# Seven 1 MB weight buffers instead of four in the expert stage of a two-block kernel

## The chip, the cores and the metric

The kernel runs on one core of one Trainium2 chip. The metric is the device time of one launch in microseconds (us), lower is better. Three runs of the kernel before gave 2560.94, 2565.24 and 2565.53 us, median 2565.24 us.

## The reference, cut to what matters

Two blocks follow each other on 256 tokens of width 1024, everything in float32. The first block has two attentions, a cross attention and, at its end, a mixture of experts: 32 experts in 4 groups, 2 experts per token.

```
x = x + cross_attention(...)
hm = rms_norm(x, g_ffn)                      # 256 x 1024
group, two experts of it per token, weights  # the routing
y[e] = (silu(xb @ w_gate[e]) * (xb @ w_up[e])) @ w_down[e]   # 1024 -> 512 -> 1024, 32 experts
x = x + sum over the two experts of weight * y
```

The second block works on two sequences of 256 rows, the tokens (the first block's result) and a context, which does not depend on the first block at all. Per layer of two: a gated feed-forward (1024 to 2816 to 1024), a mixer (layer 0: recurrent mLSTM plus spatial gating; layer 1: window attention, whose keys and values come partly from the context), and a second feed-forward. The context stops after its keys and values of layer 1. Scales and shifts of each step come from a modulation, `silu(c) @ ada_w`.

## The kernel before, in words

Two instruction streams are recorded and then woven into one order per engine by a scheduler at compile time. `fore` is first block, routing, experts, and then the second block's token rows. `back` is the modulation weights and the context rows. Names of tiles begin with f or b after their stream. The scheduler simulates the program with its own timing and takes, among what it thinks is ready, the instruction with the lowest priority number; a stream's number is a start plus a slope times the matmul work done so far (`SEG`, line 1832). The resulting order is fixed: each engine runs its row in that order and waits on semaphores. The queue that issues all weight loads is SP's, and it too is strictly in order: a load that waits for its buffer holds up every load behind it, of either stream.

A `fore` load is 128 x 2048 floats, 1 MB, into one of the `raw` buffers (`FORE`, raw=4). A `back` load is 128 x 1024 floats, 0.5 MB, into one of five. Dense layers take float32 apart: ScalarE copies 512 columns of the raw buffer into a rounded part (tag `sph`), VectorE (for `fore`) or GpSimd (for `back`) subtracts to get the rest (tag `spl`), and TensorE does three fp32r matmuls per 128 x 128 block. A raw buffer is free again when the subtraction has read it. A 0.5 MB load of `back` feeds 24 matmuls of 256 columns.

The experts do without that: their weights go from the raw buffer straight into float32 matmuls, so an expert buffer is free when TensorE has read it (lines 1190 to 1219). Four experts of a group are done together, 32 token slots each, in 8 groups. A group is 16 loads of gate and up weights, a gate function, four transposes, 8 loads of down weights, and a combine that adds the result to `xres`. Gathers of the next tokens stand between groups. After group `SPILL` there is one extra expert with 6 loads. That is 198 loads of 1 MB. Behind the experts stands a loop for further extra experts (`tc.For_i`, line 1306), which runs zero times with these inputs; it splits the program, and what the scheduler puts ahead of it stays ahead of it.

The tags `sph`, `spl`, `q1`, `dg`, `ld`, `rope` and `wg` (splits, rotary tables, attention pieces, narrow weights) are used by the first block before the routing and by the token rows behind the loop, not by the experts. Before the change they have memory of their own throughout.

The stages in the profile: first block and routing to about 451 us, experts 451 to 1316, the loop, then on the token rows a feed-forward (full rate from 1383 to 1546), the mixer of layer 0 (to about 1817), two feed-forwards (to 2182), the window attention, and the last feed-forward.

Of the kernel before, what the change touches and what calls it, by code (L numbers as in the profile page):

```python
# [39 lines left out]
class X2:  # L40


    def __init__(self, h, l, both=None):
        self.h, self.l, self.both = h, l, both
# [27 lines left out]
class Stream:  # L72
    def __init__(self, K, es, name, bufs, ps_bufs, unit):
        self.K, self.name, self.bufs = K, name, bufs
        self.pool = es.enter_context(K.tc.tile_pool(name=name, bufs=1))
        self.pp = es.enter_context(K.tc.tile_pool(name=name + "p", bufs=ps_bufs, space=PSUM))
        self.n = self.ada = self.lows = 0
        self.sq = None
        self.pool_low = LOW.get(name)
        self.unit = unit  # L80
        self.chain, self.side = {}, {}
        self.seg(0, 1)

    def seg(self, start, slope):

        self.start, self.slope, self.done = start, slope, 0.0
# [8 lines left out]

    def t(self, tag, shape, dt=F32):
        self.n += 1
        return self.pool.tile(shape, dt, tag=tag, bufs=self.bufs[tag], name=f"{self.name}{tag}{self.n}")

    def parts(self, n=T):  # L100

# [56 lines left out]
class Kern:  # L158
    def __init__(self, tc, I, dbg=None):
        self.tc, self.real, self.I, self.dbg = tc, tc.nc, I, dbg  # L160
        self.nc = Engines(self, tc.nc)
        self.cur = self.stream = None
        self.p0 = tc.cur_priority
        self.after = {}

    def link(self, key, r):
        if self.cur is None:
            return
        for prev in (self.cur.get(key), self.after.pop(key, None)):
            if prev is None:  # L170
                continue
            self.tc.add_manual_dep(
                r.ins, prev, mybir.DependencyInfo(mybir.DependencyClass.NoSync, mybir.DependencyReason.DATA),
                reason="stream order")
        self.cur[key] = r.ins.name
# [20 lines left out]
    def pair(self, S, src):  # L196

        if S.unit == 2048:
            raw = self.load(S, src)
            return raw[:, :1024], raw[:, 1024:]  # L200
        return [self.load(S, src[:, i * 1024:(i + 1) * 1024]) for i in range(2)]

    def misc(self, S, tag, shape, src, dt=F32):
        t = S.t(tag, shape, dt)
        self.real.gpsimd.dma_start(t, src)
        return t
# [824 lines left out]
    def moe(self, S):  # L1031
# [7 lines left out]
        xx = S.t("xx", [128, 2, 2, 1024], F32R)  # L1039
# [12 lines left out]
        def ct(n):  # L1052
            used[0] += n
            return scratch[:, used[0] - n:used[0]]
# [23 lines left out]
        dg = ct(8).rearrange("p (b n) -> p b n", b=2)  # L1078
# [58 lines left out]
        def onehot(base, n, b, shift=None):  # L1137
            d = S.t("c", [128, 2])
            if shift is None:
                ts(d, dest[:, :, b], -float(base), None, op0=OP.add)  # L1140
            else:
                tt(d, dest[:, :, b], shift.to_broadcast([128, 2]), op=OP.subtract)
            o, f = S.t("k1", [128, n], F32R), S.t("k1", [128, n])
            ts(f, iota[:, :n], d[:, 0:1], None, op0=OP.is_equal)
            stt(o, iota[:, :n], d[:, 1:2], f, op0=OP.is_equal, op1=OP.add)
            return o
# [13 lines left out]
        def combine(py, s):  # L1160

            o, ws = s
            Yh, Yl = S.t("k4", [128, 1024], F32R), S.t("k4", [128, 1024], F32R)
            for i in range(2):
                q = slice(i * 512, (i + 1) * 512)
                self.split_to(Yh[:, q], Yl[:, q], py[i], ws)
            for d in range(0, KC, 2):
                p = S.ps([128, 2, T])
                for i in range(2):
                    q = slice((d + i) * 128, (d + i + 1) * 128)  # L1170
                    self.mm(p[:, i], Yh[:, q], o, True, False)
                    self.mm(p[:, i], Yl[:, q], o, False, True)
                nc.vector.tensor_tensor(xres[:, d:d + 2], xres[:, d:d + 2], p, op=OP.add)

        wg, wu, wd = I["w_eg"], I["w_eu"], I["w_ed"]

        def gather(pair):
            P = [onehot(256 * pair, 256, b) for b in range(2)]
            xg = [S.t("k4", [128, 4, T]) for _ in range(2)]
            for k in range(0, KC, 2):  # L1180
                p = S.ps([128, 2, T])
                for i in range(2):
                    q = slice((k + i) * 128, (k + i + 1) * 128)
                    for b in range(2):
                        self.mm(p[:, i], hm[b][0][:, q], P[b], b == 0, False)
                        self.mm(p[:, i], hm[b][1][:, q], P[b], False, b == 1)
                nc.scalar.activation(xg[k // 4][:, k % 4:k % 4 + 2], p, AF.Copy)
            return xg

        def experts_in(grp, xg):  # L1190
            g = grp % 2
            pg = [S.ps([128, 512]) for _ in range(2)]
            for k in range(KC):
                raws = [self.load(S, wt[grp, k]) for wt in (wg, wu)]
                for s in (1, 0):
                    for j in range(4):
                        self.mm(pg[s][32 * j:32 * j + 32],
                                xg[k // 4][:, k % 4, g * 128 + 32 * j:g * 128 + 32 * j + 32],
                                raws[s][:, j * 512:(j + 1) * 512], k == 0, k == KC - 1)
            a = self.gated(S, pg[0], 512)  # L1200
            stt(a, a, 0.5, pg[1], op0=OP.mult, op1=OP.mult)
            return a

        def experts_out(grp, a):
            pt = S.ps([128, 512])
            for c in range(4):
                nc.tensor.transpose(pt[:, c * 128:(c + 1) * 128], a[:, c * 128:(c + 1) * 128], self.ident)
            hT = S.t("k2", [128, 4, 128])
            nc.scalar.activation(hT.rearrange("p a b -> p (a b)"), pt, AF.Copy)
            py = [S.ps([128, 512]) for _ in range(2)]  # L1210
            for c in range(4):
                raws = [self.load(S, wd[grp, 2 * c + i]) for i in range(2)]
                for i in (1, 0):
                    for j in range(4):
                        self.mm(py[i][32 * j:32 * j + 32], hT[:, c, 32 * j:32 * j + 32],
                                raws[i][:, j * 512:(j + 1) * 512], c == 0, c == 3)
            slot = S.t("c", [128, 1])
            ts(slot, self.cst[:, C_PCOL:C_PCOL + 1], 128.0 * grp, None, op0=OP.add)
            combine(py, scatter(slot))

        xg = gather(0)

        ta, tb = S.t("k2", [128, 16, 32]), S.t("k2", [128, 16, 32])
# [69 lines left out]
        for grp in range(8):  # L1293
            a = experts_in(grp, xg)
            if grp % 2 == 1 and grp < 7:
                xg = gather(grp // 2 + 1)
            experts_out(grp, a)
            if grp == SPILL:
                spill(sync.value_load(ti[0:1, 0:1], min_val=0, max_val=7),
                      sync.value_load(ti[0:1, 16:17], min_val=0, max_val=3))  # L1300

        self.moe_load = S.chain["sync"]

        n_more = self.real.values_load(ti[0:1, 32:33], min_val=0, max_val=15)
        keep_chain, self.cur = self.cur, None
        with tc.For_i(0, n_more) as it:
# [516 lines left out]


SPILL = 4
DEFER = 0
PLAN = {-1: 'rrr', 0: 'r', 6: 'r', 8: 'raak'}
PLAN_N = 32
CUT = ((0, 9, 9, 9, 9), (0, 3, 3, 3, 3))
FORE = dict(raw=4, sph=3, spl=3, xx=1, k1=6, k2=4, k4=6, c=16, q1=4, dg=2, ld=1, dst=6, wg=2, gc=5, c72=1, rope=1)  # L1830
BACK = dict(raw=5, sph=3, spl=3, xh=1, xl=1, k1=4, k2=4, k4=3, c=16, q1=2, wg=1, gc=4, c72=1)
SEG = dict(c1b=(1150, 2), first=(-5000, 1), ada=(0, 0), c0a=(300, 1.25), c0b=(530, 1.3), c0c=(680, 1.3), ada1=(950, 3), c1a=(1050, 4.8),
           route=(-5000, 1), moe=(365, 2.6), tok=(1050, 1.38))
# [3 lines left out]
def kernel(ctx: ExitStack, tc: tile.TileContext, I, out, dbg=None, stop=None):  # L1837
    K = Kern(tc, I, dbg)
    nc = K.nc
    fore = Stream(K, ctx, "f", FORE, 5, 2048)  # L1840
    back = Stream(K, ctx, "b", BACK, 3, 1024)
    K.dram = ctx.enter_context(tc.tile_pool(name="dram", bufs=1, space=bass.MemoryType.DRAM))
    K.setup(fore, ctx)

    def context():
# [113 lines left out]
    for c in range(KC):  # L1959
        nc.vector.scalar_tensor_tensor(x[:, c], x[:, c], K.gains[:, 5, c:c + 1], bc, op0=OP.mult, op1=OP.mult)  # L1960
        nc.sync.dma_start(out[:, c], x[:, c])


def _units(w):
# [145 lines left out]
```

## Time and profile before

| | |
|---|---|
| median of three runs | 2565.24 us (2560.94 to 2565.53) |
| the profiled execution | 2558.79 us, its span 2557.0 us |
| TensorE busy / mean granted clock | 93% / 0.964 |
| VectorE, ScalarE, GpSimd busy | 60%, 48%, 29% |
| moved by DMA | 617.23 MB, mean 241 GB/s |

The span is what lies between the first and the last instruction. A busy TensorE is not a TensorE at its peak, since the ends of pipelined matmuls are modelled; the number of matmuls in a stretch (the x in a row) tells more. A DMA share near 1.0 means that the 16 DMA engines have no idle time left.

### The profile page before, as it was taken

What the parts mean: (1) busy time and instruction counts of PE and PEld (TensorE: products, weight loads), DVE (VectorE), ACT (ScalarE), POOL (GpSimd) and SP (SyncE); (2) the same over time, 40 slices, a digit from 0 to 9 for tenths busy, and PEclk for the clock granted to TensorE, in tenths of its full rate; (3) what the DMA queues carried; (4) which work ended last, traced back from release to release, by engine and by line L of the source; (5) the groups of instructions that cost most, each with busy time, mean ns of one, the idle gap of its engine ahead of it and who ended that gap; (6) DMA issues with size and microseconds to landing.
All of it is one profiled execution on the core that took longest, in us unless ns stands there. A gap on an engine that the chain in (4) does not pass through costs nothing. (4 is left out here: it accounts for less than half of the span.)

```text
span 2557.0 us, 46079 instructions
## 1 busy us (share of the span) xinstructions
PE 2373.3 (93%) x17688; PEld 1998.3 (78%) x17688; DVE 1533.7 (60%) x3347; ACT 1228.0 (48%) x2510; POOL 730.0 (29%) x584
## 2 busy tenths in 40 slices
PE   6999998998989999999679999998999899798998
PEld 4767998785666888878348998988899799667897
DVE  6546677235543333352148776767878777677777
ACT  4434554343433433343035555545556555565554
POOL 1000245664524665656141004231000100524000
PEclk9999998999989999999889999999999999899999
DMA  9896543997979898989884554462455355355452
GB/s 373 312 333 255 179 154 132 357 354 293 383 293 364 334 352 306 366 327 343 348 309 168 182 188 142 176 212 103 166 188 191 135 194 182 115 184 197 168 193 102
DMA packets 115231, 617.23 MB, mean 241 GB/s; under 512 B 13232, under 2 KB 14704, under 8 KB 63936
## 3 DMA queue, kind: packets, MB, share of 16 engines
q1 hardware_dynamic: 113616, 610.20, 64.4%
q0 software_dynamic: 1392, 4.06, 0.5%
q8 instruction: 140, 2.29, 0.3%
q14 instruction: 83, 0.68, 0.1%
HBM read 612.11 MB, written 2.10 MB: 240 GB/s over the span
## 5 line engine op out<-in xcount | busy, mean ns | idle before, releaser
L60 POOL TENSOR_TENSOR bspl<-braw,bsph 128x512 fp32r<-128x512 f32 x468 | 608.6, 1309 | 883.3 <-ACT bsph L60 830.4
L60 PE MATMUL fps<-fxx,fsph 128*128 128x512 f32 (+2 forms) x2656 | 734.8, 346 | 19.5 <-DVE fxx L60 10.3
L60 ACT ACTIVATE fsph<-fraw 128x512 fp32r<-128x512 f32 x764 | 479.4, 629 | 483.2 <-PE fps L60 427.9
L60 DVE TENSOR_TENSOR fspl<-fraw,fsph 128x512 fp32r<-128x512 f32 x712 | 498.6, 703 | 234.0 <-ACT fsph L60 216.7
L60 PE MATMUL fps<-fxx,fspl 128*128 128x256 f32 (+1 forms) x2000 | 571.6, 286 | 1.9 <-DVE fspl L60 1.5
L60 PEld LDWEIGHTS fps<-fxx,fsph 128*128 128x128 f32 x2656 | 467.1, 193 | 88.8 <-DVE fxx L60 16.5
L60 ACT ACTIVATE bsph<-braw 128x512 fp32r<-128x512 f32 x468 | 290.9, 629 | 389.9 <-PE bps L60 321.2
L60 PEld LDWEIGHTS fps<-fxx,fspl 128*128 128x128 f32 x2000 | 384.1, 192 | 7.5 <-DVE fspl L60 4.4
L60 PE MATMUL bps<-bxh,bsph 128*128 128x256 f32 x1264 | 363.9, 288 | 5.6 <-ACT bsph L60 3.8
L60 PE MATMUL bps<-bxh,bspl 128*128 128x256 f32 x1264 | 363.7, 288 | 4.2 <-POOL bspl L60 4.0
L60 PE MATMUL bps<-bxl,bsph 128*128 128x256 f32 x1264 | 360.5, 285 | 2.3 <-DVE fk L60 2.2
L60 PE MATMUL fps<-fk,fsph 128*128 128x256 f32 x1632 | 297.8, 284 | 0.0
L60 PEld LDWEIGHTS bps<-bxh,bsph 128*128 128x128 f32 x1264 | 243.5, 193 | 30.6 <-issue 11.9
L60 PEld LDWEIGHTS bps<-bxh,bspl 128*128 128x128 f32 x1264 | 243.1, 192 | 24.6 <-POOL bspl L60 17.3
L60 PEld LDWEIGHTS fps<-fk,fsph 128*128 128x128 f32 x1632 | 254.7, 192 | 3.8 <-issue 0.9
L60 PEld LDWEIGHTS bps<-bxl,bsph 128*128 128x128 f32 x1264 | 243.3, 192 | 10.7 <-issue 8.1
L60 POOL TENSOR_TENSOR fk<-fk,fk 128x512 f32<-128x512 f32 x16 | 21.2, 1323 | 774.2 <-ACT fk L60 769.1
L60 PE MATMUL fps<-fraw,fk 128*32 128x512 f32 (+1 forms) x1600 | 211.2, 642 | 29.9 <-DMA fraw<-in_w_eu_dram 17.9
L60 PE MATMUL fps<-fk,fspl 128*128 128x256 f32 x816 | 230.8, 283 | 0.0
L60 DVE SCALAR_TENSOR_TENSOR bk<-bk,bps 128x256 f32<-128x256 f32 (+1 forms) x148 | 60.3, 411 | 246.9 <-ACT bk L60 244.9
L60 PE MATMUL bps<-bk,bsph 128*128 128x256 f32 x1056 | 198.9, 287 | 3.7 <-DVE bk L60 1.9
L60 PEld LDWEIGHTS bps<-bk,bsph 128*128 128x128 f32 x1056 | 167.6, 194 | 14.0 <-issue 5.9
(351 smaller groups left out, 3203.4 us busy)
## 6 DMA issues: line engine op xcount, KB each, us to landing
fraw<-in_ffn_in_dram SPq DMA_DIRECT2D x88, 1024.0 KB, 4.8
braw<-in_ffn_in_dram SPq DMA_DIRECT2D x132, 512.0 KB, 5.9
fraw<-in_w_eg_dram SPq DMA_DIRECT2D x66, 1024.0 KB, 7.2
fraw<-in_w_eu_dram SPq DMA_DIRECT2D x66, 1024.0 KB, 9.2
fraw<-in_w_ed_dram SPq DMA_DIRECT2D x66, 1024.0 KB, 6.9
fraw<-in_ffn_out_dram SPq DMA_DIRECT2D x44, 1024.0 KB, 4.8
braw<-in_ffn_out_dram SPq DMA_DIRECT2D x66, 512.0 KB, 5.8
braw<-in_ada_w_dram SPq DMA_DIRECT2D x59, 512.0 KB, 7.4
```

Source lines behind the costliest of these rows:

```text
L60: r = f(*args, **kw)
```

## The change

The seven tags move from the stream's pool into a second one that is closed and opened again by phase: "f1" for the first block, "fm" for the experts, "f2" for the token rows. In "fm" the same memory holds three more 1 MB buffers, tag `more`. A new function `expert` replaces `load` in the experts' groups and takes in turn four buffers of `raw` and three of `more`. The extra expert (`spill`) and all else keep `load`. A tile of a later phase waits for the tiles of the earlier one whose memory it takes.

```diff
+    def phase(self, name, tags=()):
+        if self.scope:
+            self.scope.close()
+        self.scope, self.tags = ExitStack(), tags
+        self.extra = self.scope.enter_context(self.K.tc.tile_pool(name=name, bufs=1, side="right", reuse_waits="tile"))
...
+        pool = self.extra if tag in self.tags else self.pool
+        return pool.tile(shape, dt, tag=tag, bufs=self.bufs[tag], name=f"{self.name}{tag}{self.n}")
...
+    def expert(self, S, src):
+        raw = S.t("raw" if self.experts % 7 < 4 else "more", [128, S.unit])
+        self.experts += 1
+        self.nc.sync.dma_start(raw, src)
+        return raw
...
-                raws = [self.load(S, wt[grp, k]) for wt in (wg, wu)]
+                raws = [self.expert(S, wt[grp, k]) for wt in (wg, wu)]
...
-                raws = [self.load(S, wd[grp, 2 * c + i]) for i in range(2)]
+                raws = [self.expert(S, wd[grp, 2 * c + i]) for i in range(2)]
...
+        S.phase("fm", ("more",))
         xg = gather(0)
...
+        S.phase("f2", PHASE)
         n_more = self.real.values_load(ti[0:1, 32:33], min_val=0, max_val=15)
...
+PHASE = ("sph", "spl", "q1", "dg", "ld", "rope", "wg")
```

No arithmetic changes, but the scheduler's simulation comes out otherwise, and with it the order on every engine. Counted in the order of both programs: of `back`'s 0.5 MB loads 300 stand ahead of the loop before and 267 after; of its matmuls 5230 before and 4423 after. `fore` has the same work on both sides of the loop. Behind the loop, `back`'s matmuls up to the first ones of the token mixer are 340 before and 823 after, and within the mixer 585 before and 909 after. From the second token feed-forward on both orders have the same work.

The first place is SP's queue at the first expert loads. Before (braw are loads of the context, fraw those of `fore`; w_eg, w_eu, w_ed are gate, up and down weights of the experts):

```order
L60 DMA fraw_12255<-in_w_eg_dram 128x2048
L60 DMA fraw_12257<-in_w_eu_dram 128x2048
L60 DMA braw_1331<-in_ffn_in_dram 128x1024
L60 DMA fraw_12267<-in_w_eg_dram 128x2048
...
L60 DMA braw_1632<-in_ffn_in_dram 128x1024
L60 DMA fraw_12269<-in_w_eu_dram 128x2048
L60 DMA braw_1634<-in_ffn_in_dram 128x1024
...
L1299 TENSOR_LOAD fdst_12233
```

The same place after:

```order
L60 DMA fraw_12276<-in_w_eu_dram 128x2048
L60 DMA fmore_12286<-in_w_eg_dram 128x2048
L60 DMA fmore_12288<-in_w_eu_dram 128x2048
L60 DMA fmore_12298<-in_w_eg_dram 128x2048
L60 DMA braw_1635<-in_ffn_in_dram 128x1024
...
L1317 TENSOR_LOAD fdst_12240
```

Seven expert loads instead of four stand ahead of the read of the routing result (TENSOR_LOAD), and the three new ones stand ahead of the context's next load.

The second place is SP's queue at the end of the experts. Before:

```order
L60 DMA fraw_14145<-in_w_ed_dram 128x2048
L60 DMA fraw_14147<-in_w_ed_dram 128x2048
L60 DMA braw_14447<-in_ffn_in_dram 128x1024
L60 DMA braw_14449<-in_ffn_in_dram 128x1024
...
L60 DMA braw_14679<-in_ffn_in_dram 128x1024
L1306 COMPARE_AND_BRANCH
```

And after:

```order
L60 DMA fraw_14152<-in_w_ed_dram 128x2048
L60 DMA braw_7716<-in_ffn_in_dram 128x1024
L60 DMA fraw_14154<-in_w_ed_dram 128x2048
L60 DMA braw_7718<-in_ffn_in_dram 128x1024
...
L60 DMA braw_7873<-in_ffn_in_dram 128x1024
L1325 COMPARE_AND_BRANCH
```

Before, the context is through its second feed-forward of layer 0 and has begun with layer 1 (14447 to 14679) when the loop comes; after, it has only begun that second feed-forward of layer 0 (7716 to 7873).

The third place is SP's queue in the first token feed-forward behind the loop. Before:

```order
L60 DMA fraw_15238<-in_ffn_in_dram 128x2048
L60 DMA fraw_15304<-in_ffn_in_dram 128x2048
L60 DMA fraw_15371<-in_ffn_in_dram 128x2048
L60 DMA fraw_15437<-in_ffn_in_dram 128x2048
L60 DMA fraw_15504<-in_ffn_out_dram 128x2048
```

And after:

```order
L60 DMA fraw_15249<-in_ffn_in_dram 128x2048
L60 DMA braw_8339<-in_ffn_out_dram 128x1024
L60 DMA fraw_15315<-in_ffn_in_dram 128x2048
L60 DMA braw_8341<-in_ffn_out_dram 128x1024
L60 DMA fraw_15382<-in_ffn_in_dram 128x2048
```

The rest of the context's feed-forward is now woven into the tokens' one.

## Rows read from the trace of the kernel before

**Rows 1.** The page: TensorE's granted clock and the DMA share, 40 slices, in tenths.

```profile
PEclk9999998999989999999889999999999999899999
DMA  9896543997979898989884554462455355355452
```

**Rows 2.** Busy times by stage (stretch, length, engines' busy time, clock, DMA, GB/s).

```profile
451.00:1316.00 865.00, 796.63 (x6134) 607.40 (x6132) 314.83 (x695) 319.33 (x607) 446.01 (x349) 0.95 0.89 341
1316.00:1357.00 41.00, 33.44 (x247) 31.76 (x248) 34.83 (x71) 22.33 (x44) 29.63 (x22) 0.96 0.61 231
1357.00:1383.00 26.00, 24.43 (x149) 21.13 (x149) 21.53 (x48) 15.57 (x33) 0.94 (x1) 1.00 0.53 183
1383.00:1546.00 163.00, 162.88 (x1082) 149.93 (x1082) 127.60 (x252) 95.89 (x194) 1.49 (x2) 1.00 0.52 183
1546.00:1612.00 66.00, 63.85 (x471) 56.18 (x469) 46.08 (x104) 35.19 (x70) 32.92 (x25) 1.00 0.41 139
1612.00:1735.00 123.00, 118.20 (x951) 107.27 (x952) 83.90 (x197) 66.00 (x129) 31.79 (x29) 0.97 0.55 195
1735.00:1817.00 82.00, 73.23 (x520) 67.37 (x518) 63.08 (x142) 46.11 (x96) 9.23 (x7) 0.94 0.33 116
```

**Rows 3.** The same view, slices of 20 us within the experts.

```profile
600.00:620.00 20.00, 15.97 (x98) 8.33 (x98) 12.61 (x40) 6.36 (x14) 2.28 (x2) 0.83 0.73 286
620.00:640.00 20.00, 18.52 (x119) 13.44 (x117) 15.56 (x33) 9.89 (x19) 8.07 (x7) 0.91 0.60 229
...
700.00:720.00 20.00, 16.13 (x98) 13.59 (x102) 5.23 (x20) 6.49 (x15) 4.24 (x4) 0.74 0.59 234
...
820.00:840.00 20.00, 17.84 (x122) 13.69 (x123) 17.18 (x40) 8.78 (x19) 5.99 (x5) 0.85 0.68 264
...
880.00:900.00 20.00, 20.00 (x168) 16.77 (x164) 6.32 (x11) 8.53 (x16) 14.30 (x12) 1.00 0.97 369
...
980.00:1000.00 20.00, 19.49 (x150) 17.85 (x151) 12.68 (x26) 7.29 (x14) 12.24 (x10) 0.91 0.59 213
...
1100.00:1120.00 20.00, 19.96 (x152) 16.11 (x150) 13.84 (x33) 11.86 (x24) 9.48 (x8) 0.94 0.70 256
...
1220.00:1240.00 20.00, 15.23 (x120) 10.09 (x120) 2.63 (x6) 1.90 (x3) 5.95 (x5) 0.89 0.74 288
...
1260.00:1280.00 20.00, 10.11 (x65) 1.85 (x57) 0.00 (x0) 0.00 (x0) 0.00 (x0) 0.84 1.01 419
1280.00:1300.00 20.00, 12.50 (x64) 2.62 (x68) 3.16 (x10) 1.19 (x2) 0.00 (x0) 0.67 0.93 354
```

**Rows 4.** What SP's queue waited for, 300 to 1320 us (total, times, longest).

```profile
SPq L60 <- POOL bspl L60: 478.0, 159, 11.0
SPq L60 <- PE fps L60: 280.6, 172, 12.6
```

**Rows 5.** The timeline: expert matmuls in the tail (start, length, [idle before <- releaser]).

```profile
1259.29 3.62 PE L60 MATMUL fps<-fraw,fk 128*32 128x512 f32 x16 [3.14 <-DMA fraw<-in_w_eu_dram]
```

**Rows 6.** The timeline: two context matmuls in a full stretch.

```profile
882.02 0.28 PE L60 MATMUL bps<-bxh,bsph 128*128 128x256 f32 x1
882.14 0.28 PE L60 MATMUL bps<-bxl,bsph 128*128 128x256 f32 x1
```

**Rows 7.** The timeline of VectorE: two equal small operations in a row.

```profile
353.90 0.16 DVE L60 SCALAR_TENSOR_TENSOR fc<-fc 128x2 f32<-128x2 f32 x1
354.10 1.25 DVE L60 TENSOR_TENSOR fc<-fc,fc 128x2 f32<-128x2 f32 x1
```

**Rows 8.** GpSimd's subtractions for the context, 1546 to 1750 us (min/median/max ns).

```profile
L60 POOL TENSOR_TENSOR bspl<-braw,bsph x48: 1252/1289/1759, 1548.2 to 1750.0; 128x512 fp32r<-128x512 f32 x48
```

**Rows 9.** The timeline: the first block's last split, and SP's loads beside it.

```profile
382.78 0.33 SPq L60 DMA_DIRECT2D braw<-in_ffn_in_dram  x1
...
383.54 1.35 DVE L60 TENSOR_TENSOR fspl<-fraw,fsph 128x256 fp32r<-128x256 f32 x2
...
384.92 0.33 SPq L60 DMA_DIRECT2D fraw<-in_w_eu_dram  x1
```

More of the change, by code (lines that the diff above doesn't have):

```diff
@@ L77, in __init__ @@
         self.n = self.ada = self.lows = 0
-        self.sq = None
+        self.sq = self.scope = self.extra = None
+        self.tags = ()
         self.pool_low = LOW.get(name)
@@ L97, in t @@
         self.n += 1
-        return self.pool.tile(shape, dt, tag=tag, bufs=self.bufs[tag], name=f"{self.name}{tag}{self.n}")
+        pool = self.extra if tag in self.tags else self.pool
+        return pool.tile(shape, dt, tag=tag, bufs=self.bufs[tag], name=f"{self.name}{tag}{self.n}")
     def parts(self, n=T):
@@ L164, in __init__ @@
         self.after = {}
+        self.experts = 0
     def link(self, key, r):
@@ L1829 @@
 CUT = ((0, 9, 9, 9, 9), (0, 3, 3, 3, 3))
-FORE = dict(raw=4, sph=3, spl=3, xx=1, k1=6, k2=4, k4=6, c=16, q1=4, dg=2, ld=1, dst=6, wg=2, gc=5, c72=1, rope=1)
+FORE = dict(raw=4, sph=3, spl=3, xx=1, k1=6, k2=4, k4=6, c=16, q1=4, dg=2, ld=1, dst=6, wg=2, gc=5, c72=1, rope=1, more=3)
 BACK = dict(raw=5, sph=3, spl=3, xh=1, xl=1, k1=4, k2=4, k4=3, c=16, q1=2, wg=1, gc=4, c72=1)
@@ L1842 @@
     K.dram = ctx.enter_context(tc.tile_pool(name="dram", bufs=1, space=bass.MemoryType.DRAM))
+    fore.phase("f1", PHASE)
     K.setup(fore, ctx)
@@ L1961 @@
         nc.sync.dma_start(out[:, c], x[:, c])
+    fore.scope.close()
 def _units(w):
```

## The prediction

> **What bounds the kernel now.** I read the 40 slices of the page first: TensorE's clock is granted almost throughout, and the DMA share is 0.9 or more through most of the first half but about 0.5 in the second [rows 1]. So there are two programs with two limits, cut by the loop. The busy times by stage say the same with counts [rows 2]. From 451 to 1316 us, the experts, DMA runs at a share of 0.89 and 341 GB/s, with TensorE busy 796.63 of 865 us. In the first token feed-forward, 1383 to 1546, DMA is at 0.52 and TensorE is busy for 162.88 of 163 us.
>
> Within the experts, slices of 20 us show what a full stretch is [rows 3]: at 880 us TensorE does 168 matmuls in 20 us while DMA is at 0.97. They also show where it is not full. In seven of the slices (600, 620, 700, 820, 980, 1100, 1220) DMA falls to between 0.59 and 0.74. They lie about one expert group apart: while a group goes through its gate function, transposes and combine, four buffers fill up and the queue stops. The end is different: from 1220 on SP's order has no context load left ahead of the last expert loads, TensorE waits for each pair of expert loads (3.14 us before a burst of 3.62) [rows 5], does 65 matmuls in 20 us, and its clock drops to 0.67 [rows 3]. SP's queue waits mostly for buffers: 478.0 us for GpSimd's subtractions, which free the context's, and 280.6 us for TensorE, which mostly frees the experts' [rows 4].
>
> **Ahead of the loop.** The change removes no instruction. It moves 33 context loads of 0.5 MB (17.3 MB) and 807 context matmuls behind the loop, and it lets the experts' loads run 7 MB ahead instead of 4.
> - Bytes: 341 GB/s at a share of 0.89 is 383 GB/s at a full one [rows 2]. 17.3 MB are 45 us less in the stretch from 451 on.
> - Three more loads are issued before the routing is known, where DMA stands at a share of 0.3 to 0.4 [rows 1]: 3.1 MB, 8 us less.
> - Idle DMA: 0.11 of 865 us is 95 us, of which the seven slices hold 20 x (0.27 + 0.40 + 0.41 + 0.32 + 0.41 + 0.30 + 0.26) = 47 us. Three more buffers cover 8 us of DMA at each of the six places (600 and 620 are one): 8 + 8 + 6 + 8 + 6 + 5 = 41; I take 40. The bounds are 0, if what stops the queue is not the experts' buffers, and all 95.
>
> Together 45 + 8 + 40 = 93 us, bounds 53 and 148. TensorE does not stand against it: 6134 - 807 = 5327 matmuls at 168 in 20 us are 634 us, less than 865 - 93 = 772.
>
> The Trainium skill says otherwise on the bytes: "SBUF — State Buffer", section "SBUF: two separate sides", puts the path from HBM to one core at about 358 GB/s. By it the 341 GB/s would be 95% of all there is, and the remaining 275 MB could not take less than 767 us, a gain of at most 98. This trace does not agree as far as 20 us slices go: 369 GB/s at 880 and 419 at 1260 [rows 3].
>
> The hand-over of memory adds a wait. The new buffers take the memory of the first block's splits, and their loads stand ahead of a context load in SP's queue, so the context would starve if the memory came late. The last of these splits is done at 383.54 + 1.35 us, and SP's fourth expert load goes out at 384.92, right when a raw buffer becomes free [rows 9]. The new loads can follow a few us later, after the matmuls that read the split. The context load that follows them went out at 382.78 or later before; I cost this at nothing, at most the 8 us above. On the other side of the loop the splits wait for the last expert matmuls, which the token rows need anyway.
>
> **Behind the loop.** A context matmul takes 0.12 us in a full stretch (starts at 882.02 and 882.14 [rows 6]), so 807 of them are 97 us. The work comes in two pieces, by the order.
> - 483 matmuls, 58 us, up to the token mixer. The feed-forward from 1383 to 1546 has no gap, so they lengthen it by their own time. Ahead of it, 149 matmuls from 1357 to 1383 are 18 of 26 us [rows 2]; I take 6 us as filled. That leaves 52, bounds 50 and 58.
> - 324 matmuls, 39 us, in the mixer. By counts at 0.12 us, its three stretches have 66 - 57, 123 - 114 and 82 - 62 us, 38 us in all, not filled [rows 2]; some matmuls there are longer, so this is an upper bound. I take half of the 39 as hidden: 19 us, bounds 0 and 39.
>
> Together 71 us, bounds 50 and 97.
>
> What could make the mixer worse is its chain of small VectorE operations. In the routing, where GpSimd subtracts for the context, two equal small operations in a row took 0.16 and 1.25 us [rows 7], and a subtraction on GpSimd takes 1289 ns [rows 8]. 324 matmuls bring 27 subtractions, each worth up to 1.1 us on that chain: up to 30 us, which is why the upper bound lets nothing be hidden. The same page and section of the Trainium skill says that VectorE and GpSimd share a pair of ports which one holds for a whole instruction while the other is blocked; the trace agrees with 1.25 beside 0.16 us. In the feed-forward it does not decide: VectorE's 127.60 us [rows 2] and 40 subtractions of 1.1 us are 172 of then 221 us.
>
> **The sum.** -93 + 71 = -22 us. The profiled execution took 2558.8 us with a span of 2557.0 and would take 2537. It lies 6.4 us under the median of the runs shown, 2565.2; against that median the forecast is 2543.
>
> **The rivals.**
> - A, slower: SP's own order keeps the queue standing. 478.0 of the 758.6 us that it waited for these two were for context buffers [rows 4], and three more expert buffers don't help a queue that is stopped by a context load in front of them. Then the dips stay, only the bytes are gained, and the token rows pay for the moved work: -53 + 71 = +18, 2583. It becomes slower from the point where less than 18 us of idle DMA are regained; with nothing hidden in the mixer it reaches -53 + 97 = +44, 2609. For it: the dips also coincide with slow stretches of the context. Against it: at 700 and 980 DMA is at 0.59 although TensorE still does 98 and 150 matmuls, and the dips come once per group.
> - B, much faster: with seven buffers the DMA has hardly an idle slice left, 75 of 95 us regained, and the thin mixer hides more: -(45 + 8 + 75) + 60 = -68, 2497. For it: TensorE needs only 634 us there, and the tail with its clock of 0.67 goes, because context work is left to fill it. Against it: the context still runs through its own chains ahead of the loop, and SP stays in order.
> - C, it doesn't do what it says: the new buffers' memory is handed over late and the context's loads behind them stand. The 8 us of early loads are lost, and about as much again for the stall: -22 + 16, 2559. Against it: the split that ends at 384.9 [rows 9].
>
> **How the numbers follow.** Forecast 0.50 (its own range 2515 to 2570), A 0.22, B 0.20, C 0.08. 0.2%, about 5 us, is what a measurement of this kernel can tell from no change. Faster by more than that holds B, most of C and of the forecast, 0.68; within it a little of the forecast, A and C, 0.10; slower most of A and the forecast's upper end, 0.22. The range takes in the middle of A and of B: 2495 to 2592.
>
> **What would show it.** In the changed profile the loop (now line 1325) should come at about 1316 - 93 = 1223 us, and the DMA share from the first expert matmul on should be 0.93 to 0.95 without dips under 0.7. There should be no stretch like 1260 to 1300 with some 65 matmuls in 20 us and a lowered clock. Between the loop and the token mixer there should be some 480 more context matmuls and about 52 us more, in the mixer some 20 us more, and the last 740 us, from the second token feed-forward on, should be as before. If the stretch ahead of the loop is shorter by 55 us or less, A holds and the kernel is slower; if by over 120, B. If SP stands for more than some us on a `more` load near 390 us, it is C. A mixer that grows by 39 us or more would show that I was wrong in hiding half of the moved work.

## The result, and the profile after

The changed kernel took 2528.15 us against 2565.24 before, ratio 0.9856 [0.9841, 0.9871]. A second run of it on another chip gave 2530.04 us, ratio 0.9871 [0.9854, 0.9887]. The forecast was 2543, range 2495 to 2592, faster. The profile shown here is that of the second run, since the first one's is of an execution of 4552.62 us in which TensorE's matmuls took longer throughout (those of the costliest group 561 ns each instead of 345, with the clock recorded as granted in full). Its span is 2529.1 us, 27.9 less than that of the profile before; by medians the gain is 35 to 37, so 7 us or more of it do not stand in the stages below.

The page, TensorE's clock and the DMA share in 40 slices, answers to [rows 1]:

```profile
PEclk9999999999999899998999999999999999899999
DMA  9896544999998789996455544552555355354452
```

The first half is fuller (9 where there were 8 and 7), the second half is as it was. In place of [rows 2] I cut both kernels where one stage really hands over to the next: the first expert matmul, the end of the last combine, the end of the first token feed-forward, the end of the mixer. Columns: stretch, length, TensorE's busy time and matmul records, clock, DMA share, GB/s. Before:

```profile
451.70:1313.00 861.30, 793.20 (x6112) 0.95 0.89 342
1313.00:1546.10 233.10, 223.58 (x1499) 0.99 0.53 189
1546.10:1782.00 235.90, 226.01 (x1772) 0.99 0.46 160
1782.00:2557.00 775.00, 722.11 (x4922) 0.96 0.47 167
```

The changed kernel, the same four stages:

```profile
438.00:1186.70 748.70, 699.54 (x5358) 0.96 0.92 368
1186.70:1475.40 288.70, 281.26 (x1976) 0.97 0.55 188
1475.40:1753.70 278.30, 264.30 (x2068) 0.98 0.48 162
1753.70:2529.10 775.40, 718.65 (x4939) 0.96 0.47 167
```

The experts end 126.3 us earlier (1186.7 instead of 1313.0), 13.7 of it because they start earlier. Of that, 55.6 us are given back in the feed-forward and 42.4 in the mixer; the stretch behind them is the same to 0.4 us. Nearly four fifths of what was won ahead of the loop is paid again behind it.

Where did the experts' time go? TensorE's waits there, before (who waited, for what; total, times, longest):

```profile
PE fps L60 <- DMA fraw<-in_w_eu_dram: 17.9, 8, 3.8
PE bps L60 <- DVE bk L60: 13.8, 10, 2.9
PE bps L60 <- ACT bk L60: 11.7, 10, 3.0
PE fps L60 <- DMA fraw<-in_w_ed_dram: 11.3, 5, 4.8
```

and the first three of the changed kernel:

```profile
PE bps L60 <- DVE bk L60: 14.6, 13, 2.7
PE bps L60 <- ACT bk L60: 11.4, 8, 3.0
PE bps L60 <- POOL bspl L60: 5.9, 7, 0.9
```

Of the 29.2 us in which TensorE waited for expert weights, the wait of [rows 5], 1.9 are left. What stands first now are the context's own chains, much as they were. SP's queue, 300 to 1190 us, answers to [rows 4]: less for TensorE (280.6 before), little less for the subtractions (478.0).

```profile
SPq L60 <- POOL bspl L60: 433.3, 136, 17.1
SPq L60 <- PE fps L60: 179.9, 129, 10.3
```

Slices of 20 us, with TensorE, weight loads, VectorE, ScalarE, GpSimd, clock, DMA share and GB/s as in [rows 3]:

```profile
860.00:880.00 20.00, 17.08 (x107) 11.97 (x108) 14.42 (x40) 7.21 (x15) 5.04 (x4) 0.74 0.54 184
880.00:900.00 20.00, 20.00 (x152) 16.16 (x151) 8.82 (x18) 8.15 (x16) 9.21 (x8) 0.91 0.57 198
...
1120.00:1140.00 20.00, 20.00 (x166) 15.29 (x166) 3.90 (x9) 7.01 (x12) 12.50 (x10) 1.00 1.01 413
1140.00:1160.00 20.00, 18.16 (x135) 14.62 (x135) 7.20 (x16) 7.31 (x15) 11.13 (x9) 0.91 1.00 403
1160.00:1180.00 20.00, 17.90 (x138) 11.95 (x136) 7.21 (x23) 7.31 (x14) 12.66 (x11) 0.92 0.38 121
```

The tail with 65 matmuls in 20 us and a clock of 0.67 has gone: there are 135 and 138. Dips of the DMA remain, 0.54 at 860 and 0.57 at 880. And the hand-over of memory, SP's queue where [rows 9] were read (start, length, load):

```profile
372.20 0.33 SPq L60 DMA_DIRECT2D fraw<-in_w_eu_dram  x1
374.91 0.33 SPq L60 DMA_DIRECT2D fmore<-in_w_eg_dram  x1
375.34 0.37 SPq L60 DMA_DIRECT2D fmore<-in_w_eu_dram  x1
375.80 0.39 SPq L60 DMA_DIRECT2D fmore<-in_w_eg_dram  x1
377.82 0.33 SPq L60 DMA_DIRECT2D braw<-in_ffn_in_dram  x1
```

The three `more` loads go out within 1.3 us, and the context's next load 2 us behind them, earlier than the 382.78 of before. Nothing stood.

Two slips in what stands ahead of the prediction, on which no number rests. The context loads that move are those of its first feed-forward of layer 1, not of its second of layer 0. And counting whole 0.5 MB loads alone, 299 stood ahead of the loop and now 266 (300 and 267 with a quarter-size one).

### The profile page after: what moved, and what is told of

Its sections match the earlier page's. It is cut to its first block, busy times and chain, and to the rows that moved or that the text cites. A ratio compares the mean times of both kernels' runs of the same rounds, so it can differ in the third digit from the quotient of the medians.

```text
span 4550.8 us, 46066 instructions
## 1 busy us (share of the span) xinstructions
PE 4462.1 (98%) x17688; PEld 3606.1 (79%) x17688; DVE 1487.9 (33%) x3347; ACT 1237.6 (27%) x2510; POOL 722.4 (16%) x584
## 4 chain that ended last, share of the span: by engine, by line
PE 53%; DVE 1%; issue 0%; ACT 0%; DMA 0%; DVEq 0%; ACTq 0%
PE fps L60 42%; PE bps L60 10%; DVE fk L60 0%; DVE fxx L60 0%; DVE fc L60 0%; DVE bxl L60 0%; DVE xres L60 0%; DVE bk L60 0%; DMA braw<-in_ada_w_dram 0%; ACT fk L60 0%; ACT fsph L60 0%; ACT fxx L60 0%; DVE braw L60 0%; DVEq L2127 0%; ACT bk L60 0%
## 5 line engine op out<-in xcount | busy, mean ns | idle before, releaser
L60 PE MATMUL fps<-fxx,fsph 128*128 128x512 f32 (+2 forms) x2656 | 1332.5, 561 | 10.3 <-DVE fk L60 6.8
L60 PEld LDWEIGHTS fps<-fxx,fsph 128*128 128x128 f32 x2656 | 785.7, 324 | 214.7 <-issue 185.4
L60 PE MATMUL fps<-fxx,fspl 128*128 128x256 f32 (+1 forms) x2000 | 880.5, 440 | 0.0
L60 PEld LDWEIGHTS fps<-fxx,fspl 128*128 128x128 f32 x2000 | 641.9, 321 | 12.5 <-issue 6.9
L60 PE MATMUL bps<-bxh,bsph 128*128 128x256 f32 x1264 | 563.9, 446 | 4.0 <-DVE bk L60 1.7
L60 PE MATMUL bps<-bxh,bspl 128*128 128x256 f32 x1264 | 563.4, 446 | 0.7 <-POOL bspl L60 0.7
L60 PE MATMUL fps<-fk,fsph 128*128 128x256 f32 x1632 | 541.8, 439 | 0.0
L60 PEld LDWEIGHTS fps<-fk,fsph 128*128 128x128 f32 x1632 | 475.0, 348 | 9.7 <-issue 7.7
L60 PEld LDWEIGHTS fps<-fk,fspl 128*128 128x128 f32 x816 | 282.7, 346 | 0.0
L60 PE MATMUL bps<-bk,bspl 128*128 128x256 f32 x528 | 234.9, 445 | 2.7 <-POOL bspl L60 2.7
```

The source lines that it names most:

```text
L60: r = f(*args, **kw)
```

## The experiments

Twelve runs, each against the kernel before on the same chip. Stages are read as above, in us; "ahead" are the context's whole loads and its matmuls ahead of the loop, counted in the order; the last two columns are TensorE's busy time over the kernel and what is left of the span.

| run | median, ratio [95%] | ahead | experts start, end | feed-forward | mixer | busy, left |
|---|---|---|---|---|---|---|
| before | 2565.24 | 299, 5230 | 451.7, 1313.0 | 233.1 | 235.9 | 2373.3, 183.7 |
| changed, again | 2530.04, 0.9871 [0.9854, 0.9887] | 266, 4423 | 438.0, 1186.7 | 288.7 | 278.3 | 2358.1, 171.0 |
| five buffers | 2541.22, 0.9905 [0.9885, 0.9926] | 299, 5229 | 439.3, 1284.1 | 233.0 | 250.5 | 2360.8, 178.6 |
| seven, kept order | 2564.20, 0.9995 [0.9979, 1.0011] | 299, 5230 | 437.8, 1312.0 | 232.0 | 247.3 | 2366.1, 195.7 |
| four, work moved | 2610.97, 1.0191 [1.0174, 1.0209] | 267, 4454 | 450.9, 1269.1 | 294.0 | 271.3 | 2386.6, 220.7 |
| split alone | 2552.49, 0.9945 [0.9924, 0.9965] | 299, 5230 | 437.4, 1316.6 | 231.4 | 240.7 | 2369.0, 190.1 |
| first seven loads | 2545.78, 0.9925 [0.9896, 0.9954] | 299, 5229 | 437.6, 1296.7 | 231.2 | 242.1 | 2355.4, 185.7 |
| six buffers | 2521.63, 0.9821 [0.9795, 0.9847] | 276, 4661 | 439.6, 1209.0 | 295.9 | 244.4 | 2351.6, 169.9 |
| seven, 279 loads | 2538.27, 0.9890 [0.9869, 0.9910] | 279, 4741 | 437.5, 1240.8 | 286.3 | 240.1 | 2374.7, 163.1 |
| seven, 277 loads | 2558.50, 0.9977 [0.9967, 0.9987] | 277, 4690 | 438.0, 1250.2 | 295.3 | 239.1 | 2396.3, 159.1 |
| six, 282 loads | 2546.64, 0.9931 [0.9915, 0.9948] | 282, 4826 | 439.6, 1252.2 | 275.3 | 244.0 | 2368.1, 175.6 |
| 277, whole fours | 2551.68, 0.9953 [0.9936, 0.9970] | 275, 4658 | 443.0, 1236.6 | 297.3 | 244.1 | 2375.7, 173.9 |
| seven, whole fours | 2527.10, 0.9862 [0.9838, 0.9885] | 271, 4550 | 444.8, 1204.4 | 310.2 | 240.0 | 2356.6, 169.5 |

**The changed kernel again.** No edit. Expected:

> The changed kernel once more, for a profile at the usual speed (the one that came with the result ran with TensorE at about half its rate throughout). Theory (the prediction's sum): stretch ahead of the loop shorter by about 93 us, up to 130 because the time fell by 37 us and not by 22; between loop and mixer +52 us, mixer +19 us; total near 2528. Rival B: the stretch ahead is shorter by 120 us or more and the piece behind the loop costs what was said. Rival 'cheap behind the loop': ahead -93, behind only about +55.

It repeats the gain and gives the stages that the others are held against. Ahead of the loop it is past the 120 us of rival B, behind it past all that was expected.

**Depth without moved work (five buffers).** `% 5 < 4` and `more=1`: the order keeps 299 loads ahead of the loop. Expected:

> Five expert buffers (one `more` instead of three). The order leaves as much context work ahead of the loop as before the change (299 loads of 0.5 MB, 5229 matmuls), so only the depth changes. Theory (depth covers idle DMA at the six group ends, 2.7 us of DMA for each buffer): 6 x 2.7 + 2.7 early = -19 us, 2546. Rival A (the queue stands on the context's loads, depth is worth nothing): 2565. Rival 'the gain is the moved work': 2565, since nothing moved.

2541 us, near the theory's 2546. The split and the fifth buffer together give about two thirds of the whole gain with no work moved: the experts end 28.9 us earlier, and nothing is paid in the feed-forward. But over half of it is not depth at all: the split alone (below) gives some 14 of these 24 us by the ratios, and the two intervals just overlap.

**Seven buffers, order kept.** The last group's loads are held in SP's queue behind the context's last ones:

```diff
         late(PLAN.get(-1, ""))
+        K.hold = back.chain["sync"]
...
+            if grp == 7:
+                self.after["sync"] = self.hold
             a = experts_in(grp, xg)
```

Expected:

> Seven buffers, but the last expert group's loads are held in SP's order behind the context's loads that stood ahead of the loop before the change (299 loads and 5230 matmuls ahead again). Theory (depth 48 us, moved work 45 us less ahead and 71 more behind): 2565 - 48 = 2517, faster than the changed kernel. Rival 'the gain is the moved work, which leaves something to fill the end of the experts': the end of 24 expert loads is bound by DMA alone again, at most 20 us gained, 2545 to 2565.

My theory missed by 47 us, and the rival's range held the time. Its last 50 us slices within the experts, columns as for the 20 us slices:

```profile
1150.00:1200.00 50.00, 45.06 (x332) 43.44 (x333) 22.35 (x52) 23.01 (x44) 32.86 (x26) 0.87 0.43 137
1200.00:1250.00 50.00, 50.00 (x418) 48.43 (x417) 18.01 (x30) 24.99 (x46) 44.81 (x35) 1.00 0.68 234
1250.00:1300.00 50.00, 31.88 (x210) 11.02 (x209) 4.91 (x14) 1.83 (x3) 1.85 (x2) 0.83 1.01 419
```

The experts run ahead, then TensorE works off the context with DMA at 0.43, and then the last expert group runs alone at full DMA with TensorE 32 of 50 us busy. In this order depth only moved the idle time, since the two streams did not stay mixed.

**Moved work without depth (four buffers).** The context's last piece (the line that ends `context()`) is recorded behind the experts in the kernel before:

```diff
-        late(PLAN.get(-1, ""))
...
     steps = tokens()
+    K.cur, K.stream = back.chain, back
+    K.after["sync"] = K.moe_load
+    late(PLAN[-1])
```

Expected:

> Four buffers as before, but the context's first feed-forward of layer 1 is recorded behind the loop (267 loads and 4454 matmuls ahead, as after the change, 1899 matmuls behind). Theory: -45 us of bytes ahead, nothing of the idle DMA, +71 behind: 2565 + 26 = 2591. Rival 'the gain is the moved work': 2530 to 2545.

1.9% slower, slower than theory and rival said. Ahead of the loop it is as the theory had it (43.9 us earlier, forecast 45); behind it the moved work cost 96.3 us and not 71. The experts, the feed-forward and the mixer of it, columns as in the stages above:

```profile
450.90:1269.10 818.20, 716.39 (x5341) 0.92 0.88 339
1269.10:1563.10 294.00, 287.05 (x2020) 0.98 0.55 190
1563.10:1834.40 271.30, 258.35 (x2022) 0.97 0.47 160
```

and TensorE's first waits in the experts:

```profile
PE fps L60 <- DMA fraw<-in_w_eu_dram: 38.3, 15, 5.5
PE fps L60 <- DMA fraw<-in_w_ed_dram: 23.1, 10, 5.0
```

TensorE is rid of 76.8 us of work and gets 33.7 us of idle time and a lower granted clock (0.92 instead of 0.95) for it: its waits for expert weights double from 29.2 to 61.4 us, with the context gone that stood between. The stage is shorter by 43 us, which is what the 32 loads are worth in bytes (the forecast had 45 for 33). Behind the loop the moved matmuls cost as much as with seven buffers: +60.9 and +35.4. This kernel also lacks the split of the memory, so what lies between it and the changed kernel, 82 us by the ratios, is not depth alone.

**The split of the memory alone.** `expert` always takes `raw`, nothing else is changed from the changed kernel. Expected:

> The memory of the phases is split as in the changed kernel, but the experts keep four buffers; 299 context loads stand ahead of the experts' loop, as in the kernel before. Theory: the 14 us that the changed kernel gained ahead of the first expert matmul, and about 12 us of what it lost in the mixer, come from the split alone and cancel: first expert matmul at 438, expert stage 861, mixer 248, about 2563 us. Rival (the 14 us come from the three expert loads that start early): first expert matmul at 452, about 2577 us. Rival (the split does nothing; both come with the deeper buffers): 2565 us with every stage as in the kernel before.

All three theories missed: 2552.5 us, 13 us less than before. Its profiled execution, 2560.9 us, was the longest of four (the others 2550.7 to 2552.6), so its stages show only that the experts start at 437.4, as in all kernels with the split, without ending earlier. The earlier start is partly work put off: ahead of the first expert matmul stand 34 context matmuls fewer (1464 records instead of 1498). It is won early in the first block, ahead of any expert load: the 901st matmul record of `fore` starts at 219.5 us before, at 203.8 here and at 203.4 in the changed kernel. So some 14 us are won with no deeper buffer. What brings them is open.

**Only the first seven loads.** `% 7 < 4 or self.experts >= 7`. Expected:

> Seven buffers for the first seven expert loads, four after that: only the early start of three loads is left of the depth; 299 context loads ahead of the loop, as before. Theory: the run with the split alone, less 8 us at the start of the expert stage (three loads of 1 MB at 383 GB/s): expert stage 853, about 2555 us. Rival (the depth of the first loads decides how the whole expert stage runs): expert stage 845 as with five buffers, about 2545 us. Rival (the early loads take the DMA from the context's loads and give nothing): as the split alone, 2563 us.

2545.8 us, 7 us under the split alone where 8 were worked out for three early loads; but the two intervals overlap, so this is not shown. The time is also that of the first rival (2545), but not its expert stage of 845: this one takes 859.1.

**Six buffers.** `% 6 < 4`, `more=2`. Expected:

> Six buffers; 276 context loads ahead of the loop (before 299, changed kernel 266), 568 context matmuls more behind it than before (changed kernel 806). Theory (gain in proportion to the loads that move and to the buffers, loss in proportion to the matmuls that move): start -14, bytes 23 x 1.37 = -31, depth two thirds of the changed kernel's 69 = -46, first token feed-forward 0.70 x 56 = +39, mixer 12 + 0.70 x 30 = +33: about 2546 us. Rival (the moved matmuls cost what they cost, and the depth beyond five gives nothing more): 2560 us. Rival (the sixth buffer already gives all of the 69): 2520 to 2525 us.

2521.6 us, as the rival had it in which the sixth buffer gives all of the depth, and the lowest median here; its ratio of 0.9821 [0.9795, 0.9847] lies below that of seven buffers in the second run and overlaps with the first, 0.9856 [0.9841, 0.9871], by a little. The three stages:

```profile
439.60:1209.00 769.40, 719.18 (x5580) 0.97 0.92 365
1209.00:1504.90 295.90, 288.43 (x2065) 0.98 0.54 192
1504.90:1749.30 244.40, 229.16 (x1772) 0.97 0.44 154
```

The experts end 22 us later than with seven, but the mixer has none of the moved work (1772 records, as before) and is 34 us shorter.

**More context work ahead of the loop.** The slope of the experts' stream in the simulated order (`moe`) goes from 2.6 to 3.2 and 3.0 with seven buffers, and to 3.4 with six, so that the context's work comes earlier. Expected, in this order:

> Seven buffers as in the changed kernel, but the order is simulated with context work given earlier during the experts, so that 279 context loads and 4741 of its matmuls stand ahead of the loop (changed kernel 266 and 4423, before 299 and 5229). Theory (depth and moved work add): start -14, bytes 20 x 1.37 = -27, depth -69, first token feed-forward 0.61 x 56 = +34, mixer 12 + 0.61 x 30 = +30: about 2519 us, better than the changed kernel. Rival (the depth pays only while no context load stands in the queue ahead of the experts' loads, so it falls with the work that is left ahead): expert stage 775 to 790, about 2535 us or more.

> Seven buffers with context work given a little earlier in the simulated order, so that 277 context loads and 4690 of its matmuls stand ahead of the loop: the same split of work as the run with six buffers (276 and 4661). Theory (the split of the context's work decides, and the seventh buffer adds the few us by which the end of the expert stage of the changed kernel lay below that with six, at equal loads): 2512 to 2522 us, first token feed-forward +59 (539 matmuls x 0.11), mixer as before. Rival (work given earlier fills TensorE in the middle of the experts and the depth drains there, as in the run with 279 loads, whose DMA fell to 198 GB/s at 900 to 950): 2530 to 2540 us.

> Six buffers with context work given earlier in the simulated order: 282 context loads and 4826 of its matmuls ahead of the loop (with six buffers as run before, 276 and 4661). Theory (moved matmuls cost 0.11 us each behind the loop, loads 1.37 us each ahead of it, the depth of six keeps its worth): 2521.6 + 6 x 1.37 - 165 x 0.11 = about 2512 us. Rival (the depth pays only while the order leaves TensorE room in the middle of the experts, so it falls with work given earlier): 2530 to 2540 us.

None was faster than with the slope of 2.6: with 277 and 282 loads the kernels were clearly slower, with 279 (0.9890) the interval overlaps with that of the changed kernel. The theory that depth and moved work simply add fell three times (by 19, 36 and 35 us over its value or its upper end); two of the rivals' ranges were passed as well. With 277 loads, nearly the split of work that was best with six buffers, the kernel was some 40 us slower than that one by the ratios. TensorE's busy time tells where: 2396.3 us over the kernel instead of 2351.6, for the same matmuls. A stretch of its timeline:

```profile
974.59 1.04 PE L60 MATMUL fps<-fmore,fk 128*32 128x512 f32 x2
975.57 0.39 PE L60 MATMUL bps<-bxh,bspl 128*128 128x256 f32 x1
...
976.02 0.28 PE L60 MATMUL bps<-bxh,bspl 128*128 128x256 f32 x1
976.23 1.05 PE L60 MATMUL fps<-fmore,fk 128*32 128x512 f32 x2
```

and how the expert matmuls stand in the changed kernel:

```profile
999.43 1.93 PE L60 MATMUL fps<-fraw,fk 128*32 128x512 f32 x16
1001.28 0.39 PE L60 MATMUL bps<-bxh,bspl 128*128 128x256 f32 x1
```

An expert matmul leaves two records and uses 32 of TensorE's columns. In the changed kernel eight of them, two groups of four on different columns, take 1.85 us to the next matmul; in the other a single one takes 0.98. Four abreast cost about what one costs. (The Trainium skill, "TensorEngine Tiling (Array Packing)", section "Key Properties", says that tiles work independently and in parallel; the traces agree, 1.85 us for eight beside 0.98 for one.) Where the simulated order lets context matmuls trickle in between, a group of four pays several times. Counted in the order, as steps of one to four neighbours on different columns, the 792 expert matmuls ahead of the loop take 201 steps before and with six buffers, 202 in the changed kernel, 222, 242 and 215 in these three.

**Whole fours.** The second to fourth matmul of a group get a priority ahead of all others in the simulated order: in the run with 277 loads, and in the changed kernel.

```diff
-        return self.K.p0 + 10000000 + int(1000 * (self.start + self.slope * self.done))
+        return self.K.p0 + (0 if self.tight else 10000000 + int(1000 * (self.start + self.slope * self.done)))
...
+        if self.stream is not None and out.shape[0] == 32:
+            self.stream.tight = self.quad % 4 > 0
+            self.quad += 1
         self.nc.tensor.matmul(out, lhsT, rhs, start=start, stop=stop, **kw)
         if self.stream is not None:
+            self.stream.tight = False
```

Expected:

> The run with seven buffers and 277 context loads (2558.5 us), with one more rule for the simulated order: the second to fourth matmul of each group of four expert matmuls (32 columns of TensorE each, 128x32 by 128x512) come ahead of any context matmul. In the order, the 792 expert matmuls ahead of the loop then take 212 steps instead of 242 (201 in the kernel before; a step is one to four of them on different columns, next to each other); 275 loads and 4658 context matmuls stand ahead of the loop. Theory (a step costs about 1.0 us whether it holds one matmul or four, and the torn groups are what the run with 277 loads lost): 30 steps less, 2558.5 - 30 = about 2528 us, TensorE's busy time over the kernel 2366 (there 2396, with six buffers 2352). Rival (context work given earlier drains the buffers, whole groups or not): 2545 to 2560 us.

> The changed kernel with that rule for the groups of four and nothing else: 271 context loads and 4550 of its matmuls ahead of the loop (changed kernel 266 and 4423, six buffers 276 and 4661), 201 steps ahead of the loop (202). Theory (TensorE's busy and idle time make up the whole; a moved matmul costs on TensorE behind the loop what it cost ahead of it, a little more in the mixer, where about half of the changed kernel's matmuls would now stay away): between six buffers and the changed kernel, 2521 to 2527 us. Rival (the seventh buffer costs by itself): as the changed kernel, 2530 us or more. Rival (fewer moved matmuls leave TensorE waiting for less, so that it beats both): under 2516 us.

The expert matmuls of the run with 277 loads (out<-in, records | busy us, mean ns | idle before):

```profile
L60 PE MATMUL fps<-fraw,fk 128*32 128x512 f32 x936 | 149.5, 626 | 1.8 <-DMA fraw<-in_w_eu_dram 1.8
L60 PE MATMUL fps<-fmore,fk 128*32 128x512 f32 x648 | 103.1, 624 | 1.4 <-ACT fk L60 1.4
```

and of the same with whole fours:

```profile
L60 PE MATMUL fps<-fraw,fk 128*32 128x512 f32 x936 | 131.0, 615 | 0.6 <-DMA fraw<-in_w_eu_dram 0.6
L60 PE MATMUL fps<-fmore,fk 128*32 128x512 f32 x648 | 90.7, 629 | 0.8 <-ACT fk L60 0.8
```

252.6 us became 221.7, 31 us for 30 steps less: the price of a step is as the theory had it. But the time fell by 7 us, not 30, into the rival's range, and the two intervals overlap. TensorE's busy time fell by 20.6 and what is left of the span rose by 14.8: most of the freed time became waiting, so the torn groups are not all that work given earlier costs. What the rest is stays open. In the changed kernel, where hardly a group was torn (202 steps), the rule moved 5 loads back ahead of the loop, and 2527.1 us lies at the upper end of the theory (2521 to 2527). Its interval takes in the changed kernel's ratios, so this run does not tell the theory from the rival in which the seventh buffer costs by itself. Its feed-forward takes in all of the moved work, +77.1 us for 679 matmuls, and the mixer none (+4.1).

## Why the prediction was right or wrong

The sign and the time were right, 2543 forecast and 2528 to 2530 measured. The two halves were each too small, by 33 and 27 us, and these errors cancelled: that the time came out so near is in part luck.

- **Ahead of the loop, -93 forecast, -126.3 measured,** inside its bounds of 53 and 148 but past the 120 at which the text had given it to rival B. By the stage rows above, 861.3 us at 342 GB/s and a share of 0.89 became 748.7 us at 368 GB/s and 0.92. *Bytes, -45, and early loads, -8:* right together; the stage moves 275.5 MB instead of 294.6, and at 384 GB/s, a full share before, that is 50 us. With four buffers 32 moved loads shortened it by 43. What the early loads do by themselves is not told apart (7 us between two runs whose intervals overlap). *Idle DMA, -40:* right in size too; the idle share is 95 us before and 60 after, 35 less, though dips stay and 0.93 to 0.95 was not reached.
- **What failed in that part are two terms put at nothing.** The sum kept 383 GB/s for a full share, but the changed kernel gets 400 (368 at 0.92), worth 28 us on its bytes. This goes with the depth: 385 with four buffers and moved work (339 at 0.88), 397 with six (365 at 0.92); why is open. And the 13.7 us by which the experts start earlier come with the split, which I had cost at nothing. Together 50 + 35 + 28 + 14 = 127, to the rounding of the rows. The terms also do not simply add: moved work alone ended the experts 43.9 us earlier, the fifth buffer (with the split) 28.9, seven with the order kept 1.0, seven with moved work 126.3. Seen from TensorE, 93.7 us of matmuls went and 18.9 us of idle time, and its waits for expert weights fell although the context's work was no longer at hand to fill them.
- **"TensorE does not stand against it":** wrong in its reading. I took 6134 matmuls at 168 in 20 us for 730 us of need and the rest for room. The busy time of 796.63 in [rows 2] was the better number: busy time per record stayed the same (0.1298 and 0.1306 us), and the stage shrank with the records.
- **The feed-forward, +52 forecast, +55.6 measured,** bounds 50 and 58: right, with its price of 0.12 us a matmul from [rows 6]. In the runs where the moved work stays in this stage it is 0.105 to 0.115 us each by the order (+42.2 for 403, +53.2 for 488, +62.8 for 568, +77.1 for 679).
- **The mixer, +19 forecast, +42.4 measured:** wrong, by the text's own mark of 39. The step that failed is "I take half of the 39 as hidden". Hardly any was: TensorE was busy 226.0 of 235.9 us there already, and it is busy 38.3 us longer now; its idle time rose by 4.1. I had read room from counts at 0.12 us each, though some matmuls there are longer, as the text said. The other worry, VectorE's chain beside GpSimd's subtractions [rows 7, 8], did not decide it, since idle time hardly rose. (The two operations of [rows 7] are not the same one, but the reading holds: the same TENSOR_TENSOR took 0.16 us at 353.51, and a subtraction of GpSimd ran from 354.06 for 1.26 us.) With the mixer free of moved work, in the ten kernels with the split, it still took 3 to 15 us longer than before: the same 1772 matmul records take 2 to 7 us more busy time, at a granted clock of 0.95 to 0.97 instead of 0.99, and the rest is idle time. What starts this is open. Against those kernels the moved work costs 28 to 39 us in the mixer, so up to some 11 of its 39 may be hidden.
- **Behind the loop together:** +98.0 against +71, one us past the upper bound of 97.
- **The rivals.** A fell: the depth paid, and its condition (55 us or less ahead of the loop) was far off. But its mechanism is real where the order makes it so, as with seven buffers and the kept order, which gained nothing. B was passed at its mark ahead of the loop, but not by its mechanism: 35 us of idle DMA were regained and not 75, and its hidden mixer was not there. C fell: the loads go out at 374.91 and nothing stands behind them.
- **The Trainium skill's rule** that the path from HBM gives about 358 GB/s ("SBUF — State Buffer", section "SBUF: two separate sides") would, as an estimate from that figure, have had the 275 MB take 767 us or more. The stage took 748.7 at a mean of 368 GB/s, and 413 in the slice at 1120. On this one core, the measurement decides against it.

So the sum in one line: each kernel here does the same matmuls, TensorE is busy for 92 to 94% of the span, and moving a matmul across the loop mostly moves its time, about 0.12 us. What the change wins is what TensorE no longer waits (12.7 us less outside its busy time by the table) and what its matmuls take less (15.2 us of busy time, of which the experts' matmuls, 208.8 to 203.4 us, are 5.4; the rest is not taken apart). Seven buffers were not faster than six, though no run changes the seventh alone: the order differs too. By the stages the kernel with seven ends the experts 22 us earlier and the feed-forward is 7 us shorter, but 324 of the matmuls that it moves lie in the mixer, which is 34 us longer.

## What to carry to other kernels

The feed-forward and the mixer, where TensorE was busy for 96% of the time, had hardly any room: price work moved into such a stretch at its whole duration, and don't count room as matmuls times the shortest duration. A rate worked out at one depth of buffers may not hold at another. Deeper buffers paid here where TensorE waited for a load and the order kept the two streams mixed: seven buffers, with the split, were worth 35 us in one order and nothing in another. Where buffers change what a simulated order does, look at what it does to the neighbours too, such as matmuls that share TensorE only while they stand next to each other.

## What the hardware showed that I had not expected

- A lone expert matmul on 32 columns keeps TensorE 0.98 us, eight in two groups of four 1.85 us; taking 30 steps out of the order took 30.9 us off their busy time.
- DMA held 419 GB/s over 50 us at a share of 1.01 in the run with the kept order. At a full share the expert stage got 384 GB/s before (342 at 0.89) and 400 with seven buffers (368 at 0.92), worked out from the stage rows.
- Between its bursts in the tail of [rows 3], TensorE's granted clock fell to 0.67; with 135 and 138 matmuls in the same time in the changed kernel it was 0.91 and 0.92.
